# A two-layer mLSTM, sparse-attention and retention block: the mLSTM gate chain moved one section earlier, and evacuations given the weight chunks' priority

## The chip, the cores and the metric

The kernel runs on one core of one Trainium2 chip. The metric is the device time of one execution in microseconds (us); the time of a kernel is the median of its runs.

## What is computed

A sequence of 512 tokens of width 1024 goes through two layers. Each layer multiplies the normed tokens by one wide matrix `w_in`, cuts the result into the inputs of three mixers (an mLSTM, a sparse attention with an indexer, a retention), mixes, projects, and ends in a gated feed-forward block. Cut to what the change touches:

```python
h = rms_norm(x, norm1_g);  z = h @ w_in          # m_q m_k m_v m_i m_f m_o a_... r_... g_...
qk = silu(causal_conv(concat([m_q, m_k])))
# mLSTM gates, per head and token, in chunks of 128 tokens
log_f = log_sigmoid(m_f + m_fbias);  log_i = m_i + m_ibias
bcum = cumsum(log_f)                             # inside a chunk
m_row = max(bcum + m_state, max_r(bcum_l - bcum_r + log_i_r))
w_intra = exp(d_log - m_row);  w_inter = exp(bcum + m_state - m_row)
out = num / max(|den|, exp(-m_row));  m_state = max(b_last + m_state, max(g_log))
# indexer: 8 heads of scores that pick each token's keys
idx_sc = sum_g w_idx[g] * relu(q_idx[g] @ k_idx^T);  sel = top_k(idx_sc)
```

## The kernel before

All large products are made as three TensorE products of 32-bit halves (lines 251 to 253, `mm3`): a value x is held as a rounded part hi and a remainder lo, and hi*hi, hi*lo and lo*hi are added up in PSUM. Weights come in chunks of 256 rows by 512 columns (`chunk`, line 223): SP issues the load into `raw` (2 buffers), ACT writes `whi` (line 233), DVE subtracts to get `wlo` (line 234). `whi` and `wlo` have 3 buffers each. The whole of `chunk` is emitted under `tc.high_priority()`.

The work is written as sections, each 96 products of 512 columns into four `mm` PSUM tiles: `tok_section` (output rows are tokens) and `feat_section` (output rows are features). At its end a section calls `finish` (line 279), which evacuates the four tiles (on ACT or DVE, as the section says) and then runs the rest of each evacuation. The next section needs the same four PSUM tiles again.

Small work is fed in between: `self.feed` holds generators, and a section calls `tick` (line 116) eight times, which steps each generator by its rate. The program's order is only a start: Tile's scheduler orders each engine's instructions by priority and readiness, and `high_priority` lifts instructions. After that, every engine runs its list strictly in order and waits on semaphores.

The sections that matter here, in each layer: the misc section (the gate columns m_i, m_f, the indexer's inputs; line 413), QK (line 455), m_v (line 458), m_o (line 471), then r_q, r_k, r_v, r_g. Fed in between, before the change:

- in QK and m_v: `indexer` (line 607). For each of 4 head pairs `q_pair` (line 590) makes a product `sm`, from which ACT and DVE write the two `qs` tiles (lines 602, 603); for each head there are then six PE products (lines 623, 624), three ReLUs on ACT (line 626) and three accumulations into `mask` on DVE (lines 629, 631);
- in m_v: `conv_silu` (line 434): per feature tile one product and three shifted accumulations `cy` (lines 437, 440) on DVE, a Sigmoid on ACT (line 442), and `qz` or `kT` on DVE (lines 446, 448);
- in m_o: `mlstm_pre` (line 752) and `topk` (line 636), the latter at lowered priority. `mlstm_pre` begins with the gate chain: eight PE transposes of `gates` (lines 760, 761), 23 small DVE instructions on 4 partitions (lines 762 to 785), an Exp and a Ln on ACT (lines 765, 766) and, at the end, another Exp (line 787); then the PE transposes of the results A, nm and wl (line 793), the decay weights `mw` (lines 800 to 805), `qw` and `kw` (lines 811 to 823).

The small products use four `sm` PSUM tiles; POOL multiplies the four `og` tiles by the gain at the end of m_o (line 466).

Of the kernel before, what the change touches and what calls it, by code (L numbers as in the profile page):

```python
# [11 lines left out]
F32 = mybir.dt.float32  # L12
F32R = mybir.dt.float32r
AF = mybir.ActivationFunctionType
OP = mybir.AluOpType
# [88 lines left out]
class Block:  # L104
# [172 lines left out]
            self.finish(evac, [p[:, 0:n] for p in ps])  # L277

    def finish(self, evac, ps):
        rest = [evac(i, p) for i, p in enumerate(ps)]  # L280
        for f in rest:
            if f:
                f()
# [91 lines left out]
    def mixer(self, l, act):  # L375
        nc, a = self.nc, self.a
        w_in = a["w_in"][l]
        small = self.small[l]
        ib, conv = self.load_small(l)
# [3 lines left out]
        gates = self.st.tile([128, NT, 8], F32, name="gates", bufs=2)  # L383
# [37 lines left out]
        qz = self.b8("qz", [4, T])  # L421
# [32 lines left out]
        self.during((idx, 0.9), (bias, 0.6))  # L454
        self.feat_section(w_in, ((C_QK, C_QK + 512),), act, ev_qk)
        cs = conv_silu()
        self.feed.append([cs, 0.5, 0.0])
        self.tok_section(w_in, ((C_MV, C_MV + 512),), act, ev_v)
        self.drain(idx, bias, cs)

        mg = self.gain(a["m_norm_g"][l]).rearrange("p (h v) -> p h v", h=4)
        og = [self.r(f"og{t}", [4, 128]) for t in range(NT)]
# [2 lines left out]
            nc.scalar.activation(og[t], ps.rearrange("p (h v) -> p h v", h=4), AF.Sigmoid)  # L465
            nc.gpsimd.tensor_mul(og[t], og[t], mg)

        pre = self.mlstm_pre(l, gates, ib, qz, kT)
        top = self.topk(masks)
        self.during((pre, 1.0), (top, 1.0))  # L470
        self.tok_section(w_in, ((C_MO, C_MO + 512),), act, ev_og)
# [120 lines left out]
    def q_pair(self, W, f, CT, scale, t0):  # L592
        nc = self.nc
        p = self.sm()[:, 0:T - t0]
        for k in range(2):
            self.mm3(p, [x[:, k, f * 128:(f + 1) * 128] for x in W], [x[:, k, t0:] for x in CT], k == 0, k == 1)
        out = []
        for s in range(2):
            q = self.r("qs", dtype=F32R)
            d = q[:, t0:]  # L600
            hi, lo = (slice(0, 64), slice(64, 128))[::1 - 2 * s]
            nc.scalar.activation(d[hi], p[hi], AF.Copy, scale=scale)
            nc.vector.scalar_tensor_tensor(d[lo], p[hi], scale, d[hi].bitcast(F32), op0=OP.mult, op1=OP.subtract)
            out.append(q)
        return out

# [142 lines left out]
            self.to_T(ha[b].rearrange("p (f d) -> p f d", f=4), haT, b)  # L749
            yield  # L750

    def mlstm_pre(self, l, gates, ib, qz, kT):
        nc = self.nc
        g1, g2 = self.b8("g1", [4, T]), self.b8("g2", [4, T])
        li, fb, e, B = (g1[0:4, i, :] for i in range(4))
        A, M, nm, wl = (g2[0:4, i, :] for i in range(4))
        wi = e
        pi, pf = self.sm(), self.sm()
        for t in range(NT):
            nc.tensor.transpose(pi[0:4, t * 128:(t + 1) * 128], gates[:, t, 0:4], self.ident)  # L760
            nc.tensor.transpose(pf[0:4, t * 128:(t + 1) * 128], gates[:, t, 4:8], self.ident)
        nc.vector.tensor_scalar(li, pi[0:4], ib[:, 0:1], None, op0=OP.add)
        nc.vector.tensor_scalar(fb, pf[0:4], ib[:, 1:2], None, op0=OP.add)
        nc.vector.scalar_tensor_tensor(e, fb, -1.0, fb, op0=OP.mult, op1=OP.min)
        nc.scalar.activation(e, e, AF.Exp)
        nc.scalar.activation(e, e, AF.Ln, bias=1.0)
        nc.vector.scalar_tensor_tensor(fb, fb, 0.0, e, op0=OP.min, op1=OP.subtract)
        rows = [self.r("rows", parts=36, dtype=F32R) for _ in range(2)]
        for x in rows:
            nc.gpsimd.memset(x.bitcast(F32), 0.0)  # L770
        keep = self.r("keep", parts=4)
        nc.vector.memset(keep, 1.0)
        nc.vector.memset(keep[:, 0::128], 0.0)
        nc.vector.tensor_tensor_scan(B, keep, fb, 0.0, op0=OP.mult, op1=OP.add)
        nc.vector.tensor_sub(A, li, B)
        m = self.st.tile([4, NT + 1], F32, name="g_ms", bufs=2)
        nc.vector.memset(m[:, 0:1], 0.0)
        for c in range(NT):
            s = slice(c * 128, (c + 1) * 128)
            last = (c + 1) * 128  # L780
            nc.vector.tensor_tensor_scan(M[:, s], A[:, s], A[:, s], m[:, c:c + 1], op0=OP.max, op1=OP.max)
            nc.vector.tensor_add(m[:, c + 1:c + 2], B[:, last - 1:last], M[:, last - 1:last])
            nc.vector.tensor_scalar(wi[:, s], M[:, s], -1.0, m[:, c:c + 1], op0=OP.mult, op1=OP.add)
            nc.vector.tensor_scalar(wl[:, s], A[:, s], M[:, last - 1:last], None, op0=OP.subtract)
        nc.vector.scalar_tensor_tensor(nm, B, -1.0, M, op0=OP.mult, op1=OP.subtract)
        self.split(rows[0][0:4], rows[0][32:36], M)
        nc.scalar.activation(wi, wi, AF.Exp)
        self.split(rows[1][0:4], rows[1][32:36], wi)
        yield
        tok = self.sm([128, 3, NT, 4])  # L790
        for i, r in enumerate((A, nm, wl)):
            for c in range(NT):
                nc.tensor.transpose(tok[:, i, c, :], r[:, c * 128:(c + 1) * 128], self.ident[0:4, 0:4])
        G = self.st.tile([128, 3, NT, 4], F32, name="g_tok", bufs=2)
        nc.vector.tensor_copy(G[:, 0], tok[:, 0])
        nc.scalar.activation(G[:, 1:3], tok[:, 1:3], AF.Exp)
        W = self.b8("mw", [NT, 4, 128])
        for h in range(4):
            p = self.sm()
            nc.tensor.matmul(p, lhsT=self.sel[:, h:h + 1].to_broadcast([36, 128]), rhs=rows[0], start=True, stop=True)  # L800
            d = W[:, :, h, :]
            nc.vector.tensor_sub(d, self.negT[:, None, :].to_broadcast([128, NT, 128]),
                                 p.rearrange("p (c l) -> p c l", c=NT))
            for c in range(NT):
                nc.scalar.activation(W[:, c, h, :], W[:, c, h, :], AF.Exp, bias=G[:, 0, c, h:h + 1])
            yield
        qw = self.b8("qw", [4, T])
        dec = self.st.tile([128, 2, NT], F32, name="g_dec", bufs=2)
        for hp in range(2):
            p = self.sm()  # L810
            nc.tensor.matmul(p, lhsT=self.pair[:, hp * 128:(hp + 1) * 128], rhs=rows[1], start=True, stop=True)
            for s in range(2):
                nc.vector.tensor_mul(qw[:, 2 * hp + s, :], qz[:, 2 * hp + s, :], p)
            nc.vector.tensor_copy(dec[:, hp, :], p[:, 127::128])
            yield
        kw = [self.r(f"kw{c}", [4, 128]) for c in range(3)]
        for c in range(3):
            nc.gpsimd.memset(kw[c], 0.0)
            p = self.sm([128, 2, 2, 64])
            for hp in range(2):  # L820
                nc.tensor.transpose(p[:, hp].rearrange("p s d -> p (s d)"), kT[hp][:, c * 128:(c + 1) * 128], self.ident)
            for s in range(2):
                nc.vector.tensor_mul(kw[c][:, s::2, 64 * s:64 * s + 64], p[:, :, s, :],
                                     G[:, 2, c, s::2, None].to_broadcast([128, 2, 64]))
            yield
        self.ml = (W, G, qw, kw, dec)
# [196 lines left out]
```

## Time and profile before

| | us |
|---|---|
| median of 3 runs (lowest, highest) | 1836.69 (1836.31, 1838.33) |
| the profiled execution | 1840.39 |
| its span, first to last instruction | 1838.5 |
| PE busy in the span | 1803.9 (98%) |
| DVE busy | 985.8 (54%) |
| ACT busy | 733.1 (40%) |
| POOL busy | 215.1 (12%) |

Busy time of PE counts overlapping, pipelined products, so that 98% does not say that PE works at its peak; what PE waits for is read from its waits, and how fast it goes from the granted clock. "Idle before" in a row is the time in which the engine stood still just before that instruction, with what ended it.

### The profile page before, as it was taken

The numbers are of one execution on the slowest core, as the hardware profiler recorded it, in microseconds if no ns is written. First come the engines' busy times: TensorE is split into PE (matmuls) and PEld (weight loads), VectorE is DVE, ScalarE is ACT, GpSimd is POOL, SyncE is SP. The second block draws the span as 40 slices with busy tenths as digits, with TensorE's granted clock in tenths as the row PEclk, the third lists the DMA queues.
The fourth block names the chain that finished last, engine by engine and source line by source line (L and its number), as shares of the span: only waits on it lengthen the run. The fifth ranks groups of instructions, "written<-read, shape, count | busy, mean of one in ns | idle before, by whom it ended". The sixth has DMA issues, their size and how long they took to land.

```text
span 1838.5 us, 22889 instructions
## 1 busy us (share of the span) xinstructions
PE 1803.9 (98%) x8720; PEld 1497.9 (81%) x8720; DVE 985.8 (54%) x1798; ACT 733.1 (40%) x1202; POOL 215.1 (12%) x274
## 2 busy tenths in 40 slices
PE   9989999999999999999999899999999999999998
PEld 6868888878888888888888688888888888888886
DVE  5788985455555333322357889844546443333223
ACT  5553234656434233322246523356554342323221
POOL 3112240121000000000020131401210000000000
PEclk9989999999999999999999899999999999999999
DMA  5522423232235333222342223233223243332232
GB/s 186 201 85 65 119 75 98 84 94 88 81 126 149 104 92 101 94 94 102 101 130 81 63 81 103 65 98 94 89 70 120 98 150 103 92 101 94 92 103 81
DMA packets 126846, 185.95 MB, mean 101 GB/s; under 512 B 12257, under 2 KB 71137, under 8 KB 126737
## 3 DMA queue, kind: packets, MB, share of 16 engines
q1 hardware_dynamic: 125408, 178.98, 31.1%
q0 software_dynamic: 1184, 5.26, 0.8%
q8 instruction: 68, 1.11, 0.2%
q14 instruction: 42, 0.34, 0.1%
q10 hardware_dynamic: 144, 0.26, 0.0%
HBM read 177.64 MB, written 6.84 MB: 100 GB/s over the span
## 4 chain that ended last, share of the span: by engine, by line
PE 58%; DVE 7%; DMA 1%; ACT 1%; issue 1%; POOL 1%; SPq 0%; POOLq 0%; ACTq 0%; DVEq 0%
PE mm L253 18%; PE mm L251 18%; PE mm L252 18%; DVE wlo L234 2%; DVE mask L647 1%; DVE top L646 1%; PE sm L728 1%; DMA raw<-w_up 1%; PE sm L707 1%; ACT whi L233 1%; PE sm L721 0%; DVE ru L521 0%; PE sm L368 0%; POOL lnr L308 0%; PE sm L345 0%
## 5 line engine op out<-in xcount | busy, mean ns | idle before, releaser
L234 DVE TENSOR_TENSOR wlo<-raw,whi 128x1024 fp32r<-128x1024 f32 (+2 forms) x302 | 373.1, 1236 | 587.6 <-ACT whi L233 587.3
L233 ACT ACTIVATE whi<-raw 128x1024 fp32r<-128x1024 f32 (+2 forms) x302 | 313.9, 1040 | 727.8 <-PE mm L252 296.2
L251 PE MATMUL mm<-hT,whi 128*128 128x512 f32 (+1 forms) x1216 | 465.3, 383 | 1.6 <-ACT fg L956 1.6
L252 PE MATMUL mm<-hT,whi 128*128 128x512 f32 (+1 forms) x1216 | 460.4, 379 | 1.0 <-DVE hT L303 1.0
L253 PE MATMUL mm<-hT,wlo 128*128 128x512 f32 (+1 forms) x1216 | 460.8, 379 | 0.0
L253 PEld LDWEIGHTS mm<-hT,wlo 128*128 128x128 f32 x1216 | 228.7, 188 | 43.3 <-DVE wlo L234 0.2
L251 PEld LDWEIGHTS mm<-hT,whi 128*128 128x128 f32 x1216 | 228.9, 188 | 42.9 <-ACT fg L956 2.0
L252 PEld LDWEIGHTS mm<-hT,whi 128*128 128x128 f32 x1216 | 229.0, 188 | 42.0 <-DVE hT L303 1.6
L251 PE MATMUL mm<-whi,hT 128*128 128x512 f32 (+1 forms) x448 | 178.5, 399 | 1.0 <-ACT whi L233 0.4
L253 PE MATMUL mm<-whi,hT 128*128 128x512 f32 (+1 forms) x448 | 177.9, 398 | 0.0
L252 PE MATMUL mm<-wlo,hT 128*128 128x512 f32 (+1 forms) x448 | 176.9, 395 | 0.0
L253 PEld LDWEIGHTS mm<-whi,hT 128*128 128x128 f32 x448 | 85.8, 191 | 17.7 <-issue 0.9
L251 PEld LDWEIGHTS mm<-whi,hT 128*128 128x128 f32 x448 | 85.7, 191 | 17.7 <-ACT hT L302 1.4
L252 PEld LDWEIGHTS mm<-wlo,hT 128*128 128x128 f32 x448 | 85.7, 191 | 17.5 <-issue 1.3
L320 POOL TENSOR_SCALAR rs<-ms 128x1 f32<-128x1 f32 x16 | 5.7, 355 | 619.3 <-ACT hn L318 619.3
L253 PE MATMUL mm<-whi,fa 128*128 128x512 f32 x192 | 75.6, 394 | 0.0
L251 PE MATMUL mm<-whi,fa 128*128 128x512 f32 x192 | 75.5, 393 | 0.0
L252 PE MATMUL mm<-wlo,fa 128*128 128x512 f32 x192 | 75.5, 393 | 0.0
L709 POOL TENSOR_TENSOR cmb<-tb,mask 128x256 f32<-128x256 f32 (+2 forms) x48 | 52.0, 1088 | 163.1 <-DVE amx L712 74.3
L251 PE MATMUL mm<-whi,fr 128*128 128x512 f32 x160 | 62.4, 390 | 0.0
L253 PE MATMUL mm<-whi,fr 128*128 128x512 f32 x160 | 62.3, 389 | 0.0
L252 PE MATMUL mm<-wlo,fr 128*128 128x512 f32 x160 | 62.3, 389 | 0.0
(285 smaller groups left out, 2652.3 us busy)
## 6 DMA issues: line engine op xcount, KB each, us to landing
raw<-w_in SPq DMA_DIRECT2D x104, 512.0 KB, 3.6
raw<-w_gate SPq DMA_DIRECT2D x96, 256.0 KB, 2.9
raw<-w_up SPq DMA_DIRECT2D x96, 256.0 KB, 3.1
raw<-w_down SPq DMA_DIRECT2D x44, 512.0 KB, 3.5
raw<-w_out SPq DMA_DIRECT2D x16, 512.0 KB, 4.5
x<-x SPq DMA_DIRECT2D x8, 512.0 KB, 5.8
rot<-c_rot SPq DMA_DIRECT2D x16, 256.0 KB, 2.7
tb<-bias_dram SPq DMA_DIRECT2D x16, 256.0 KB, 3.4
```

Of the source, the lines that this page charges most:

```text
L233: nc.scalar.activation(h, r, AF.Copy)
L234: nc.vector.tensor_sub(o, r, h.bitcast(F32))
L251: t.matmul(out, lhsT=A[0], rhs=B[0], start=start, stop=False)
L252: t.matmul(out, lhsT=A[0], rhs=B[1], start=False, stop=False)
L253: t.matmul(out, lhsT=A[1], rhs=B[0], start=False, stop=stop)
L320: nc.gpsimd.tensor_scalar(r, ms[:, 0:1], ms[:, 1:2], EPS, op0=OP.add, op1=OP.add)
L646: nc.vector.max(m8, acc)
L647: nc.vector.match_replace(acc, m8, acc, TAKEN)
L707: nc.tensor.matmul(p, lhsT=q[v][:, b * 128:(b + 1) * 128], rhs=kk[v][:, 0:SP], start=v == 0, stop=v == 1)
L709: nc.gpsimd.tensor_add(c, tb[:, T - S:T], masks[b] if b else self.neg)
L728: nc.tensor.matmul(o[:, b, :], lhsT=PT[:, s, :], rhs=V[s][:, h * 64:(h + 1) * 64], start=s == 0, stop=s == b)
```

## The change

`mlstm_pre` is cut in two. Its first part, up to the split of the row tiles, becomes `mlstm_gates`, a generator with yields after the Ln, after A, and after each of the four chunks; it is fed at rate 1.0 in the m_v section (and drained after it), beside `indexer`, `bias_table` and `conv_silu`. The second part, from the transposes at line 793 on, stays in m_o. The arithmetic is the same. Besides, `finish` emits all evacuations under `tc.high_priority()`, and so does `q_pair` for its two evacuations.

```diff
     def finish(self, evac, ps):
-        rest = [evac(i, p) for i, p in enumerate(ps)]
+        with self.tc.high_priority():
+            rest = [evac(i, p) for i, p in enumerate(ps)]
...
         cs = conv_silu()
-        self.feed.append([cs, 0.5, 0.0])
+        rec = self.mlstm_gates(gates, ib)
+        self.feed += [[cs, 0.5, 0.0], [rec, 1.0, 0.0]]
         self.tok_section(w_in, ((C_MV, C_MV + 512),), act, ev_v)
-        self.drain(idx, bias, cs)
+        self.drain(idx, bias, cs, rec)
...
-        pre = self.mlstm_pre(l, gates, ib, qz, kT)
+        pre = self.mlstm_pre(qz, kT)
...
-            nc.scalar.activation(d[hi], p[hi], AF.Copy, scale=scale)
-            nc.vector.scalar_tensor_tensor(d[lo], p[hi], scale, d[hi].bitcast(F32), op0=OP.mult, op1=OP.subtract)
+            with self.tc.high_priority():
+                nc.scalar.activation(d[hi], p[hi], AF.Copy, scale=scale)
+                nc.vector.scalar_tensor_tensor(d[lo], p[hi], scale, d[hi].bitcast(F32), op0=OP.mult, op1=OP.subtract)
...
-    def mlstm_pre(self, l, gates, ib, qz, kT):
+    def mlstm_gates(self, gates, ib):
         nc = self.nc
+        yield
         g1, g2 = self.b8("g1", [4, T]), self.b8("g2", [4, T])
...
         nc.scalar.activation(e, e, AF.Ln, bias=1.0)
+        yield
...
         nc.vector.tensor_sub(A, li, B)
+        yield
...
             nc.vector.tensor_scalar(wl[:, s], A[:, s], M[:, last - 1:last], None, op0=OP.subtract)
+            yield
...
         self.split(rows[1][0:4], rows[1][32:36], wi)
-        yield
+        self.recur = (A, nm, wl), rows
+
+    def mlstm_pre(self, qz, kT):
+        nc = self.nc
+        (A, nm, wl), rows = self.recur
         tok = self.sm([128, 3, NT, 4])
```

What the scheduler makes of it, at three places. Line numbers of the change are higher than before by 1 to 11 (793 is 804 there, 602 is 605, 765 is 769).

PE, layer 0, around the transposes of the gate chain's last results (`sm<-cm,g`). Before, eight of the twelve stand behind the fifth product of r_q:

```order
L251 MATMUL mm<-whi,hT_117 128x512
L252 MATMUL mm<-wlo,hT_117 128x512
L793 MATMUL sm<-cm,g_1011 128x4 x8
L253 MATMUL mm<-whi,hT_119 128x512
L251 MATMUL mm<-whi,hT_117 128x512
L800 MATMUL sm<-rows,sel 128x512 x3
```

Now all twelve stand behind the 33rd product of m_o, just behind the indexer's last score products (lines 626, 627 of the change):

```order
L253 MATMUL mm<-whi,hT_119 128x512
L626 MATMUL sm<-CT_220,qs 128x384
L627 MATMUL sm<-CT_221,qs 128x384
L626 MATMUL sm<-CT_220,qs 128x512
L627 MATMUL sm<-CT_221,qs 128x512
L804 MATMUL sm<-cm,g_727 128x4 x12
L251 MATMUL mm<-whi,hT_117 128x512
```

They moved up by 68 products; the first four had stood behind the 74th product of m_o. In layer 1 four stand behind product 38 and eight behind product 57 of m_o, where they were behind 74 and 101. The eight transposes at the chain's head, which stood behind the 12th product of m_o, stand behind the 24th of m_v.

DVE, layer 0: the middle of the gate chain (`g`, `keep`), before, in the m_o section, among the first top-k steps (`top`, lines 646 and 647):

```order
L234 TENSOR_TENSOR wlo<-raw,whi 128x1024
L767 SCALAR_TENSOR_TENSOR g_1010<-g_1010 4x512
L647 MATCH_REPLACE mask_434<-top,mask_434 128x256
L774 SCALAR_TENSOR_TENSOR g_1010<-keep,g_1010 4x512
L646 MAX top<-mask_434 128x8
L775 TENSOR_TENSOR g_1011<-g_1010 4x512
L647 MATCH_REPLACE mask_434<-top,mask_434 128x256
L781 SCALAR_TENSOR_TENSOR g_1011<-g_1011,g_ms 4x128
```

and now, in the m_v section, among score accumulations (`mask`, line 634) and the remainders `qs` (line 606) of the indexer's third head pair:

```order
L234 TENSOR_TENSOR wlo<-raw,whi 128x1024
L772 SCALAR_TENSOR_TENSOR g_726<-g_726 4x512
L634 SCALAR_TENSOR_TENSOR mask_434<-relu,wgt,mask_434 128x256
L606 SCALAR_TENSOR_TENSOR qs<-sm,qs 64x384
L779 SCALAR_TENSOR_TENSOR g_726<-keep,g_726 4x512
L606 SCALAR_TENSOR_TENSOR qs<-sm,qs 64x384
L780 TENSOR_TENSOR g_727<-g_726 4x512
L634 SCALAR_TENSOR_TENSOR mask_435<-relu,wgt,mask_435 128x384
```

Top-k steps stand behind the whole chain now, and the chain stands ahead of and between the two `qs` tiles. Up to the chain's last instruction (line 785) DVE has, in layer 0, the same other work behind it as it had before up to the first `kT` (line 448); in layer 1 one `wlo`, two sets of three `mask` accumulations and a `cy` more.

ACT, layer 0, m_v section: the Exp and the Ln with their table loads now stand ahead of the evacuation of the third `qs` pair (line 605), which was preceded by ReLUs and a `whi` alone:

```order
L443 ACTIVATE cz<-cy 128x512
L629 ACTIVATE relu<-sm 128x256
L629 ACTIVATE relu<-sm 128x384
L629 ACTIVATE relu<-sm 128x512
L769 ACT_TABLE_LOAD
L769 ACTIVATE g_726<-g_726 4x512
L233 ACTIVATE whi<-raw 128x1024
L770 ACT_TABLE_LOAD
L770 ACTIVATE g_726<-g_726 4x512
L629 ACTIVATE relu<-sm 128x256
L629 ACTIVATE relu<-sm 128x384
L605 ACTIVATE qs<-sm 64x384 x2
```

The list of ACT has 49 table loads in place of 43, three more in each layer. Nothing else moves much: SP's list has layer 0's two loads of `rot` (256 KB each, line 505) moved from behind the misc section's chunks to ahead of its second and behind its third chunk, and in the attention some evacuations change places with their neighbours.

## Rows read from the trace of the kernel before

**Rows 1.** The page: its head.

```profile
span 1838.5 us, 22889 instructions
```

**Rows 2.** Waits of PE, whole span: waiter <- releaser: us in total, times, longest.

```profile
PE sm L793 <- DVE g L785: 7.3, 2, 3.6
...
PE sm L793 <- DVE g L775: 2.1, 2, 1.1
...
PE mm L251 <- ACT fg L956: 1.6, 1, 1.6
```

**Rows 3.** Timeline of PE, layer 0: start, duration, engine, line, out<-in [idle before <-releaser].

```profile
100.80 0.48 PE L251 MATMUL mm<-whi,hT 128*128 128x512 f32 x1
...
116.17 0.41 PE L793 MATMUL sm<-cm,g 4*128 4x4 f32 x4 [1.05 <-DVE g L775]
...
116.84 0.39 PE L251 MATMUL mm<-whi,hT 128*128 128x512 f32 x1
...
122.53 0.39 PE L252 MATMUL mm<-wlo,hT 128*128 128x512 f32 x1
126.55 1.00 PE L793 MATMUL sm<-cm,g 4*128 4x4 f32 x8 [3.63 <-DVE g L785]
```

**Rows 4.** Stretches, layer 0: length; busy PE, PEld, DVE, ACT, POOL (instructions); PEclk; DMA.

```profile
126.60:136.80 10.20, 10.20 (x27) 6.73 (x28) 6.45 (x13) 6.23 (x9) 1.28 (x1) 0.50 0.26 77
136.80:146.00 9.20, 9.20 (x54) 7.49 (x54) 6.65 (x17) 5.45 (x16) 0.00 (x0) 1.00 0.20 60
```

**Rows 5.** Stretch of layer 1 after its second such wait, same columns.

```profile
1034.50:1048.20 13.70, 12.44 (x32) 8.03 (x33) 7.73 (x18) 7.62 (x11) 1.28 (x1) 0.50 0.19 59
```

**Rows 6.** Timeline of PE and the stretch behind it, feed-forward part of layer 0.

```profile
586.15 0.50 PE L251 MATMUL mm<-hT,whi 128*128 128x512 f32 x1 [1.61 <-ACT fg L956]
...
587.00:600.00 13.00, 13.00 (x59) 10.66 (x58) 5.26 (x6) 3.36 (x5) 0.00 (x0) 1.00 0.54 161
```

**Rows 7.** Stretches of layer 0's gate chain, its own tile `g` alone (PE, PEld, DVE, ACT).

```profile
102.90:126.50 23.60, 0.41 (x4) 0.32 (x4) 12.56 (x23) 1.89 (x3) 1.00 0.23 67
118.50:123.40 4.90, 0.00 (x0) 0.00 (x0) 4.55 (x5) 0.00 (x0) 1.00 0.39 109
```

**Rows 8.** Timeline of DVE, layer 0.

```profile
82.41 0.55 DVE L603 SCALAR_TENSOR_TENSOR qs<-sm,qs 64x384 fp32r<-64x384 f32 x1
...
99.27 3.26 DVE L631 SCALAR_TENSOR_TENSOR mask<-relu,wgt,mask 128x256 f32<-128x256 f32 x6
...
118.54 1.31 DVE L784 TENSOR_SCALAR g<-g 4x128 f32<-4x128 f32 x1
...
124.40 0.27 DVE L784 TENSOR_SCALAR g<-g 4x128 f32<-4x128 f32 x1
...
125.83 0.67 DVE L785 SCALAR_TENSOR_TENSOR g<-g,g 4x512 f32<-4x512 f32 x1
```

**Rows 9.** Timeline of POOL, layer 0.

```profile
118.42 4.02 POOL L466 TENSOR_TENSOR og<-og,gain 128x512 f32<-128x512 f32 x3 [31.39 <-ACT og L465]
```

**Rows 10.** Stretch of layer 0 that the chain moves into, all engines as in rows 4.

```profile
70.30:99.27 28.97, 28.68 (x137) 24.03 (x136) 26.47 (x40) 18.25 (x33) 2.21 (x4) 1.00 0.44 147
```

**Rows 11.** Timeline of ACT, layer 0.

```profile
108.15 1.28 ACT L765 ACT_TABLE_LOAD   x1
109.44 0.63 ACT L765 ACTIVATE g<-g 4x512 f32<-4x512 f32 x1
```

**Rows 12.** Timeline of PE, layer 0: the third `qs` pair's first use.

```profile
83.15 0.28 PE L623 MATMUL sm<-CT,qs 128*128 128x256 f32 x1
```

**Rows 13.** Top-k's last step and its first reader, layer 0: durations, first and last start.

```profile
L647 DVE MATCH_REPLACE8 mask<-top,mask x48: 397/540/678, 109.9 to 243.6; 128x256 f32<-128x256 f32 x16, 128x384 f32<-128x384 f32 x16, 128x512 f32<-128x512 f32 x16
...
L709 POOL TENSOR_TENSOR cmb<-tb,mask x24: 724/1017/1992, 274.4 to 439.4; 128x256 f32<-128x256 f32 x8, 128x384 f32<-128x384 f32 x8, 128x512 f32<-128x512 f32 x8
```

**Rows 14.** Waits of PE's weight loads for an evacuation, whole span.

```profile
PEld mm L251 <- DVE sg L481: 1.0, 2, 0.5
```

**Rows 15.** The page: DMA issues, KB each, median us from issue to landing.

```profile
rot<-c_rot SPq DMA_DIRECT2D x16, 256.0 KB, 2.7
```

## The prediction

> **What bounds the kernel now.** I read the table of busy times first: PE is busy for 98% of the span of 1838.5 us [rows 1], DVE for 54%, ACT for 40%. So only what makes PE stand still, or go slowly, is worth time. The second view is PE's waits [rows 2]. The longest is for the gate chain, `sm L793 <- g`: 7.3 us and 2.1 us, each in two waits, one per layer, together 9.4 us. The next, 1.6 us, is in the feed-forward part and is not touched. The third view is PE's timeline in layer 0 [rows 3]: PE stands 1.05 us before the first four transposes and 3.63 us before the other eight. The fourth view, the stretches [rows 4, 5], shows what follows: right behind that second wait the granted clock is 0.50, the 1.2 GHz level, for 10.2 us in layer 0 and for some 13.7 us in layer 1, and then it is 1.00 again. PE is busy for 10.2 and 12.4 us of these, so half of that, 5.1 + 6.2 = 11.3 us, is lost to the clock. A wait of 1.61 us elsewhere is followed by a clock of 1.00 [rows 6]; so among these rows only the long wait was followed by the fall. What the chain costs today is 9.4 + 11.3 = 20.7 us.
>
> **Why the chain is late.** It is one dependent line on DVE, interleaved with top-k. Its 23 instructions take 12.56 us [rows 7]. Five of them, which run while POOL multiplies `og` [rows 9], take 4.55 us: a `g` subtraction of 0.27 us takes 1.31 us there [rows 8]. The undisturbed durations of the five, from the repeats of the same lines, add up to about 1.4 us, so that the chain by itself is 12.56 - 4.55 + 1.4 = 9.4 us.
>
> **The change part by part.**
>
> *The chain leaves m_o.* PE reaches its new place for the transposes after 33 products of m_o. Before, the 13th product started at 100.80, and a product takes (122.53 - 116.84) / 25 = 0.228 us [rows 3], so the 34th would start at 100.80 + 21 x 0.228 = 105.6 us. Nothing is added to PE: the eight head transposes are only earlier, and the time up to there is the same.
>
> When is DVE through? In layer 0 the order gives it, up to line 785, the same other work as it had done before at 99.27, when the last six `mask` steps began [rows 8]. To this the chain is added: 9.4 us, by which it would end at 99.27 + 9.4 = 108.7. DVE has holes in which some of it fits: in the 28.97 us up to 99.27 it was busy for 26.47 [rows 10], so at most 2.5 us are free. The chain then ends between 106.2 and 108.7, and if ACT's turns (the Exp and the Ln, each with a table load of 1.28 us [rows 11]) leave new holes as large as the old, at 108.7 or a little later. PE would be held up by 0.6 to 3.1 us. I take 2.4 us, nearer the upper end, because the chain goes through ACT and back twice and DVE has to wait for that in order. In layer 1 the order puts more other work ahead of line 785, some 5 us (six `mask` steps of 3.26 us together [rows 8], a `wlo` and a `cy`), but PE comes to the last eight transposes 24 products later, 24 x 0.228 = 5.5 us; so 2.4 us is taken there too. Together 4.8 us, between 1.2 and 6.2.
>
> PE need not lose this at the transposes. What is queued behind the chain on DVE and ACT are the `qs` tiles: the remainder of the third pair started at 82.41 and took 0.55 us [rows 8], and PE used it at 83.15 [rows 12], with 0.2 us to spare. Now two gate activations and two table loads on ACT and five gate instructions on DVE stand ahead of it. I expect the larger part of the wait there, at the indexer's score products, in the middle of m_v, and the rest in smaller pieces behind it, at the next pair and at the transposes.
>
> *The clock.* If the new waits are pieces of 1 to 2 us, they are nearer to the 1.61 us that left the clock alone [rows 6] than to the 3.63 us that did not [rows 3]. I take no fall: 11.3 us gained. The other end is 0.
>
> *Top-k* moves behind the chain. Its last step in layer 0 starts at 243.6 and its first reader on POOL at 274.4 [rows 13], so it has 30 us to spare and costs nothing. If it were late, POOL's `cmb` and the attention would wait.
>
> *POOL's `og` products* stay and now meet the `qw` and `kw` products and the weight remainders, where DVE would lose about the same 4.55 - 1.4 = 3.2 us per layer [rows 7]. Those feed the mLSTM's first chunk, which is fed into r_q with other products between. I take 0.5 us for both layers; the ends are 0 and 6.3.
>
> *Table loads.* Six more, 1.28 us each [rows 11], 7.7 us on an engine that is 40% busy. What of it is in front of PE is in the 2.4 us above; the rest is covered by ACT's idle time, and if it were not, the evacuations of m_o and so the first products of r_q would come late. The row shows the Exp starting at 109.44, as soon as the load that started at 108.15 is done [rows 11]. The Trainium skill (ScalarE: Activation LUTs, What ACT_TABLE_LOAD costs) gives about 1.28 us for the load and 1.38 us more of draining, 2.66 us for each switch, and advises to do all calls of one set before the next, which speaks against a change that adds switches. By the load as the rows show it the sum is the one below; by that price the rival on table loads holds.
>
> *Evacuations with priority.* The only wait of this kind on PE is 1.0 us in all [rows 14], so at most 1 us is to gain; as much could be lost in the attention, whose instructions step back. I take 0. One evacuation closure issues the load of `rot`, and in layer 0 two of them move to the first misc chunks on SP's queue. Each lands in 2.7 us [rows 15] and may hold up the second chunk by anything from 0 to that; I take 0, since that chunk's evacuation stands behind the row norms on ACT anyway.
>
> **The sum.** 9.4 + 11.3 - 4.8 - 0.5 = 15.4 us less. The profiled execution took 1840.4 us with a span of 1838.5, so it would take 1825.0. It lies 3.7 us above the median of the three runs, 1836.7; 15.4 us below that median is **1821.3 us**.
>
> **The rivals.**
>
> 1. *Clean.* DVE's holes take up the chain and no new wait comes: 20.7 us less, 1816.0. For it: DVE idles 2.5 us in that stretch [rows 10]. Against it: the chain is 9.4 us, and 0.2 us of slack at the third `qs` pair. Chance 0.11.
> 2. *The clock still falls in one layer.* The new wait is in one piece of 2.4 us or more, which lies between the wait that left the clock alone and the one that did not. 5.6 us come back: 1826.9. Chance 0.16. In both layers: 11.3 us back, 1832.6. Chance 0.10.
> 3. *Slower: the whole chain lands on PE.* All 9.4 us per layer stand on DVE in front of a `qs` tile that PE needs at once, nothing is hidden, and the clock falls as before. New waits of 18.8 us take the place of 9.4, so 1836.7 + 9.4 = 1846.1. It decides from the point at which the new waits are larger than the old ones and still end in a half clock. For it: DVE is 91% busy there [rows 10]. Against it: PE goes on with weight products until the next `qs`, and the chain is spread between them by its yields. Chance 0.04.
> 4. *Table loads cost double.* Were ACT blocked for about as long again behind each load, 1.3 us more for the two loads ahead of the third `qs` pair, that is 2.6 us per layer, come on to PE: 5.2 us back, 1826.5. Against it is the start of the Exp at 109.44 [rows 11]. Chance 0.02. The Trainium skill (ScalarE: Activation LUTs, What ACT_TABLE_LOAD costs) is what would make it so; the trace disagrees with that price.
> 5. *It does not act.* The scheduler's new places bring as much wait as before, with the same clock: 1836.7. Against it: the order shows the chain's head 84 products earlier, 84 x 0.228 = 19 us. Chance 0.02.
>
> **How the numbers follow.** The forecast has what is left, 0.55. A measurement can tell about 0.2%, 3.7 us, from no change. Faster by more than that, under 1833.0: the forecast, the clean case, one falling clock, the table loads, and half of the case of two falling clocks, which lies on the border: 0.55 + 0.11 + 0.16 + 0.02 + 0.05 = 0.89. Within: 0.05 + 0.02 = 0.07. Slower: 0.04. The range reaches from the clean case with 3 us of better evacuations and mLSTM waits, 1813, to one falling clock with the upper end of the new waits and 2.7 us for `rot`, 1831. It leaves out two falling clocks, the fifth rival and the slower one, 0.16.
>
> **What would show it.** In the changed kernel's profile: PE's wait at the transposes of `g` under 1 us per layer; new waits at the score products for `qs` or for a `relu`, 1 to 2 us each, some 5 us over both layers; the granted clock 1.00 from m_v through r_q in both layers; the `g` instructions of 4 x 128 all near 0.27 us; 49 table loads of 1.28 us. It is wrong if a stretch at 0.50 stands in m_v or m_o, if one wait of PE is over 3 us, or if PE waits in r_q for `mw`, `qw` or an `og` evacuation by several us.

## The result and the profile after

The changed kernel takes 1827.92 us (median of 4 runs, 1826.73 to 1828.15), the kernel before, on the same chip, 1837.51 (1836.31 to 1839.80): a ratio of 0.9944, 95% interval 0.9932 to 0.9955. That is faster, by 9.6 us at the medians, where 15.4 were forecast; the time lies inside the range and 6.6 us above the forecast. The two profiled executions, 1840.39 and 1827.70 us, are 12.7 us apart.

The page of the changed kernel: its head, PE's busy time, and the granted clock in 40 slices.

```profile
span 1825.9 us, 22880 instructions
...
PE 1796.5 (98%) x8720; PEld 1490.9 (82%) x8720; DVE 982.5 (54%) x1798; ACT 741.1 (41%) x1208; POOL 217.5 (12%) x274
...
PEclk9999999999999999999999999999999999999999
```

PE stands still for 1825.9 - 1796.5 = 29.4 us instead of 1838.5 - 1803.9 = 34.6, and is busy for 7.4 us less. The next fence holds PE's waits over the whole span (total, times, longest), as [rows 2] does for before.

```profile
PE sm L626 <- DVE qs L606: 2.2, 2, 1.6
PE sm L626 <- ACT relu L629: 2.1, 2, 1.3
PE sm L710 <- ACT kk L692: 2.0, 4, 0.8
...
PE mm L251 <- ACT hT L303: 1.3, 1, 1.3
PE sm L873 <- DVE msc L852: 1.1, 2, 0.9
...
PE mm L251 <- ACT fg L967: 0.2, 1, 0.2
```

The transposes of the chain (L804 now) are no longer in the list. New or longer are the score products' waits for `qs` (0.7 us in before) and for a `relu`, and, in the attention, four waits for `kk`, while two for `prob`, 1.3 us in all in before, are gone. The wait for `fg` [rows 6] has fallen from 1.6 to 0.2 us. PE's timeline in layer 0 shows the first change and the new places: 1.56 us in m_v at the third pair, and in m_o the transposes directly behind the last score products.

```profile
86.24 0.38 PE L626 MATMUL sm<-CT,qs 128*128 128x256 f32 x1 [1.56 <-DVE qs L606]
...
108.43 0.44 PE L626 MATMUL sm<-CT,qs 128*128 128x384 f32 x1 [0.81 <-ACT relu L629]
...
109.46 0.71 PE L804 MATMUL sm<-cm,g 4*128 4x4 f32 x9
```

The stretches of [rows 4, 5] at the same times, all engines: the granted clock is 1.00, the 2.4 GHz level, where two of the three stood at 0.50.

```profile
126.60:136.80 10.20, 10.20 (x56) 8.75 (x55) 9.15 (x30) 10.07 (x17) 6.30 (x5) 1.00 0.30 93
136.80:146.00 9.20, 8.34 (x54) 7.18 (x53) 8.00 (x32) 2.95 (x8) 1.27 (x2) 1.00 0.21 66
1034.50:1048.20 13.70, 13.45 (x88) 11.76 (x87) 12.46 (x49) 5.61 (x15) 1.45 (x3) 1.00 0.27 80
```

In the stretch of the chain, of its own tile `g` alone (PE, PEld, DVE, ACT), 23 DVE instructions take 9.92 us, against 12.56 in [rows 7]: away from `og` the chain is nearly as short as the 9.4 us worked out. Its last instruction ends at 108.66 us, at the upper end of the 106.2 to 108.7 worked out.

```profile
73.50:108.80 35.30, 0.00 (x0) 0.00 (x0) 9.92 (x23) 1.26 (x2) 1.00 0.34 106
```

ACT's timeline in layer 0 shows why the third pair is late. Exp and Ln of the chain each load a table, and the `qs` copy, which DVE and PE wait for, starts only at 85.14, behind both; before, its remainder on DVE already ran at 82.41 [rows 8].

```profile
79.31 1.28 ACT L769 ACT_TABLE_LOAD   x1
80.60 0.63 ACT L769 ACTIVATE g<-g 4x512 f32<-4x512 f32 x1
...
82.20 1.28 ACT L770 ACT_TABLE_LOAD   x1
83.49 0.63 ACT L770 ACTIVATE g<-g 4x512 f32<-4x512 f32 x1
...
85.14 0.46 ACT L605 ACTIVATE qs<-sm 64x384 fp32r<-64x384 f32 x1
```

### The profile page after: what moved, and what is told of

Same layout as the page of the kernel before. It is cut to its first block, busy times and chain, and to the rows that moved or that the text cites. A ratio compares the mean times of both kernels' runs of the same rounds, so it can differ in the third digit from the quotient of the medians.

```text
span 1825.9 us, 22880 instructions
## 1 busy us (share of the span) xinstructions
PE 1796.5 (98%) x8720; PEld 1490.9 (82%) x8720; DVE 982.5 (54%) x1798; ACT 741.1 (41%) x1208; POOL 217.5 (12%) x274
## 4 chain that ended last, share of the span: by engine, by line
PE 78%; DVE 14%; ACT 3%; DMA 2%; issue 2%; POOL 1%; SPq 0%; POOLq 0%; ACTq 0%; DVEq 0%
PE mm L251 23%; PE mm L253 23%; PE mm L252 23%; DVE wlo L234 3%; DVE mask L650 3%; DVE top L649 2%; PE sm L731 2%; PE sm L710 1%; ACT whi L233 1%; PE sm L724 1%; DMA raw<-w_up 1%; DVE ru L523 1%; PE sm L369 1%; DVE mhx L362 0%; DMA uk<-a_wuk 0%
## 5 line engine op out<-in xcount | busy, mean ns | idle before, releaser
L251 PE MATMUL mm<-whi,hT 128*128 128x512 f32 (+1 forms) x448 | 177.2, 396 | 2.0 <-ACT hT L303 1.3
L253 PE MATMUL mm<-whi,hT 128*128 128x512 f32 (+1 forms) x448 | 174.6, 390 | 0.0
```

The source lines that it names most:

```text
L251: t.matmul(out, lhsT=A[0], rhs=B[0], start=start, stop=False)
L253: t.matmul(out, lhsT=A[1], rhs=B[0], start=False, stop=stop)
```

## The experiments

The theory at the start: the gain is the chain's move; PE's long wait at the transposes and the half clock behind it are gone, the priorities are worth little, and what is lost again are the waits at the score products. The first rival: the priorities bring a large part. The second, about the cause: the chain is not long by itself but slowed by POOL's `og` products, so that it need not move at all.

| kernel | median us | ratio to before, 95% interval |
|---|---|---|
| the whole change | 1827.92 | 0.9944, 0.9932 to 0.9955 |
| gates_only | 1833.35 | 0.9975, 0.9966 to 0.9984 |
| prio_only | 1839.18 | 1.0006, 0.9997 to 1.0015 |
| gates_finish | 1826.99 | 0.9939, 0.9927 to 0.9951 |
| gates_qpair | 1833.00 | 0.9971, 0.9960 to 0.9982 |
| no_gain_before | 1821.72 | 0.9917, 0.9903 to 0.9930 |
| long_chain | 1830.75 | 0.9968, 0.9957 to 0.9979 |
| log_sigmoid | 1825.13 | 0.9935, 0.9923 to 0.9948 |
| gates_in_qk | 1829.39 | 0.9957, 0.9945 to 0.9970 |
| gain_late | 1827.97 | 0.9946, 0.9934 to 0.9959 |
| gain_late_log | 1829.08 | 0.9956, 0.9943 to 0.9968 |
| gain_late_mv | 1835.42 | 0.9989, 0.9980 to 0.9998 |
| gain_behind | 1820.73 | 0.9915, 0.9902 to 0.9929 |

### The parts of the change, four kernels

gates_only: the change with the gates in m_v and both priorities taken out.

```diff
-        with self.tc.high_priority():
-            rest = [evac(i, p) for i, p in enumerate(ps)]
+        rest = [evac(i, p) for i, p in enumerate(ps)]
...
-            with self.tc.high_priority():
-                nc.scalar.activation(d[hi], p[hi], AF.Copy, scale=scale)
...
+            nc.scalar.activation(d[hi], p[hi], AF.Copy, scale=scale)
```

> The gate chain is fed in the m_v section; both priorities are taken out. Theory (the move of the chain is the change, the priorities are small): the granted clock is 1.00 from m_v to r_q in both layers, PE has no wait at the transposes of the chain, and the time is 1829 to 1831, about 8 us under the kernel before; the waits of 1.6 us on the fg evacuation and 1.0 us on an sg evacuation, which the whole change lost, are back. Rival (the chain in m_v only pays if the qs and the evacuations go first): waits for qs of over 3 us in m_v, the clock falls behind them, and the time is 1834 or more.

gates_qpair: the first of these two edits alone.

> The whole change without the priority of the evacuations. Theory: the waits for fg (1.6 us) and sg (1.0 us) are back: 1829.5 to 1831. Rival (the priority of the evacuations costs as much elsewhere: the first chunks at the start, the late mw Exps in layer 0 behind two alternating activation tables): the same as the whole change or faster, 1826 to 1828.

gates_finish: the second alone.

> The whole change without the priority of the q tiles. Theory: the third qs pair, behind the chain on ACT and DVE, comes later by the instructions that now go first, so PE waits for it 1 to 2 us more per layer than in the whole change: 1829 to 1831. Rival (the scheduler finds the same order without it): the same as the whole change, 1827.9 within 0.8.

prio_only: the kernel before with both priorities added.

> The kernel before with both priorities and the gate chain left where it was. Theory: the two long waits for the chain in m_o and the half clock behind them stay, and only the waits for fg and sg go, some 2 us: 1835 to 1836.5. Rival (the priorities bring a large part of the gain): under 1833.

Measured: without the evacuations' priority the move is worth only some 5 us (1833.35 and 1833.00); with it, and without the priority of the q tiles, 1826.99. On its own the priority brings nothing (1839.18). So the first theory fails in one part: the evacuations' priority is worth 5 to 6 us, though only once the chain has moved (ratios of 0.9971 without it and 0.9944 with it, intervals apart). That the q tiles' priority is worth anything the intervals do not show. The theories on the single kernels missed: gates_only lies between its theory and its rival, gates_qpair is 2 us above its theory, gates_finish is under its theory and near its rival, although its longest wait for `qs` did grow, from 1.6 to 2.1 us, and prio_only gained none of the 2 us that were expected, although the wait for `fg` is gone there. One thing that the priority costs shows in the attention: PE waits 2.1 us for `kk` in prio_only and 1.6 in gates_finish, as in the whole change, and 1.3 us for `prob` instead in before, gates_only and gates_qpair.

In gates_qpair the waits that decide are new ones at the end of m_o. Its waits of PE:

```profile
PE mm L251 <- ACT og L466: 3.5, 2, 2.0
...
PE sm L859 <- DVE kw L833: 1.4, 1, 1.4
```

PE's timeline there, in layer 0, the first product of r_q:

```profile
132.24 0.50 PE L251 MATMUL mm<-whi,hT 128*128 128x512 f32 x1 [1.99 <-ACT og L466]
```

ACT's timeline of the same kernel:

```profile
124.10 3.62 ACT L815 ACTIVATE mw<-mw,g_tok 128x128 f32<-128x128 f32 x12
...
129.03 1.26 ACT L815 ACTIVATE mw<-mw,g_tok 128x128 f32<-128x128 f32 x4
130.29 1.28 ACT L466 ACT_TABLE_LOAD   x1
131.59 2.06 ACT L466 ACTIVATE og<-mm 128x512 f32<-128x512 f32 x4
```

And its stretch right behind (length; busy PE, PEld, DVE, ACT, POOL; PEclk; DMA):

```profile
133.10:136.50 3.40, 3.40 (x10) 2.62 (x9) 1.92 (x7) 0.56 (x2) 3.40 (x5) 0.50 0.10 33
```

The 16 `mw` Exps, which had to wait for the chain before, are now ready in m_o. Without the priority they and a table load stand ahead of the four `og` evacuations, which hold PE's four product tiles; PE waits 1.99 us, and the clock falls for 3.4 us. In layer 1 the same comes behind a wait for `kw`. In the whole change `og` goes first, at a price: ACT changes its table five times within 11 us. Its timeline in the whole change:

```profile
122.92 1.28 ACT L816 ACT_TABLE_LOAD   x1
...
124.63 1.28 ACT L467 ACT_TABLE_LOAD   x1
...
127.52 1.28 ACT L816 ACT_TABLE_LOAD   x1
...
130.19 1.28 ACT L467 ACT_TABLE_LOAD   x1
...
132.10 1.28 ACT L816 ACT_TABLE_LOAD   x1
...
135.09 3.61 ACT L816 ACTIVATE mw<-mw,g_tok 128x128 f32<-128x128 f32 x12
```

The last twelve Exps end at 138.7, where in gates_qpair the last ones ended at 130.3, and PE waits up to 0.9 us for `msc` (above): the cheaper wait.

### Why the chain was late in m_o: no_gain_before

```diff
-            nc.gpsimd.tensor_mul(og[t], og[t], mg)
+            pass
```

> The kernel before, in the same order on PE, DVE and ACT around the gate chain, without POOL's eight products of og with the norm's gain: the output lacks that gain. Theory (DVE and POOL slow each other; the clock falls only behind a wait of PE that is long): the instructions of the chain beside og take 0.27 and 0.47 us instead of up to 1.59, the chain ends some 3 us earlier in each layer, the second wait of PE falls from 3.6 to about 0.5 us, the clock stays at 1.00, and 6 + 11 = 17 us are gained: 1820 to 1822, under both kernels. Rival 1 (the chain was slow by itself): its instructions and the waits stay, 1837. Rival 2 (the clock falls for another reason than the length of the wait, as the many small transposes there): the waits shrink, the clock still falls to 0.50 for 10 to 14 us, 1831.

Measured: 1821.72, as the theory had it, and under both kernels, with the chain in its old place. DVE's timeline, where [rows 8] had 1.31 us:

```profile
118.66 0.27 DVE L784 TENSOR_SCALAR g<-g 4x128 f32<-4x128 f32 x1
```

PE's waits of this kernel for the chain:

```profile
PE sm L793 <- DVE g L775: 2.1, 2, 1.1
...
PE sm L793 <- DVE g L785: 0.4, 2, 0.2
```

The 7.3 us have become 0.4, the first wait of 2.1 us is unchanged, and the granted clock shows no 0.50 ahead of the last 3.3 us, where every kernel here has some. The span is 18.6 us shorter: 6.9 of waits and 11.3 of half clock make 18.2. Both rivals fall: the chain is not slow by itself, and here the transposes without the long wait leave the clock alone.

### Can the gain be multiplied in later? gain_late, gain_late_log, gain_late_mv, gain_behind

gain_late: the kernel before, with POOL multiplying the gain into the normalised heads.

```diff
-            nc.gpsimd.tensor_mul(og[t], og[t], mg)
...
             self.head_norm(hx, og[c])
+            nc.gpsimd.tensor_mul(hx, hx, mg)
```

> The kernel before, chain left in m_o and no priority; POOL multiplies the norm's gain into the normalised heads of each mLSTM chunk, instead of into og while the chain runs. Theory (the whole loss came from POOL's products beside the chain): the chain's instructions take 0.27 and 0.47 us, the clock stays at 1.00, and it is about as fast as the kernel without the gain, 1821.7: 1820 to 1824. Rival (the same eight products cost DVE and the mLSTM's chunks as much in r_q, or each chunk's way to PE gets 1.3 us longer and PE waits for hmT): 1826 or more.

gain_late_log adds the evacuations' priority and the log of a Sigmoid (the diff of log_sigmoid, below):

> As the one with the late gain, chain in m_o, and also the evacuations' priority and the log of a Sigmoid in the chain. Theory (the wait of 1.05 us at the first transposes in each layer comes from the chain's length, and the fg wait from the evacuations' order): another 2 to 3 us less, 1817 to 1820. Rival (in m_o the og Sigmoids and the chain's Ln alternate the tables, and the evacuations' priority is worth nothing without the chain in m_v, as measured): the same as the late gain alone, within 1.5.

gain_late_mv is the change with the late gain and the log of a Sigmoid, without the q tiles' priority:

> The changed kernel with the late gain and the log of a Sigmoid, without the q tiles' priority. Theory (in the new place POOL's og products meet only work with slack, so taking them away there gains less than 1 us; the log of a Sigmoid gains 2.8, and the q tiles' priority costs 0.9): 1823 to 1825. Rival (the products beside qw, kw and the weight remainders are what is left of the loss): under 1821.

All three miss: 1827.97, 1829.08, 1835.42. In gain_late the chain's second wait is down to 0.3 us in all, as the theory had it, but the POOL product now stands between the head norm and the transposes of `hmT`, a path with less slack than I took it to have. PE's waits in gain_late:

```profile
PE sm L368 <- POOL mhx L871: 2.3, 2, 1.1
PE sm L861 <- DVE msc L840: 2.3, 2, 1.2
```

PE's waits in gain_late_log:

```profile
PE sm L369 <- POOL mhx L870: 7.5, 2, 3.8
```

and the stretch of gain_late_log behind the first of these:

```profile
175.70:179.10 3.40, 3.40 (x10) 2.68 (x9) 0.00 (x0) 0.60 (x1) 2.21 (x4) 0.50 0.66 189
```

The wait is this long because the fourth of these products is slow itself. POOL's timeline in gain_late_log, the third and the fourth:

```profile
163.03 1.30 POOL L870 TENSOR_TENSOR mhx<-mhx,gain 128x512 f32<-128x512 f32 x1 [2.49 <-DVE mdn L864]
...
171.24 3.92 POOL L870 TENSOR_TENSOR mhx<-mhx,gain 128x512 f32<-128x512 f32 x1 [2.50 <-DVE mhx L364]
```

Beside the fourth, DVE makes `ru`, `rq`, `ru` and `wlo`, each from two SBUF tiles and in its usual time (0.69 and 1.22 us). In gain_late the fourth takes 2.79 us, in gain_late_mv 3.92; in gain_late and gain_late_log the other three take 1.26 to 1.30. So the late gain meets again what it was to avoid, POOL and DVE slowing each other, this time with POOL as the one that waits. This is read from the timelines; no run isolates it.

So the rival held for gain_late. For gain_late_log the rival's time held, not its reason. What POOL's products cost in the whole change was the question of gain_late_mv; its own new wait, 7.6 us, hides that, and it stays open.

gain_behind leaves the product on `og`, on POOL, before the heads are needed, and makes it start behind the chain: a zero worked out from the chain's result is added to the gain first.

```diff
-            nc.gpsimd.tensor_mul(og[t], og[t], mg)
...
         self.drain(pre)
+        zero = self.st.tile([128, 1], F32, name="g_zero", bufs=2)
+        nc.gpsimd.tensor_scalar(zero, self.ml[1][:, 0, 0, 0:1], 0.0, None, op0=OP.mult)
+        nc.gpsimd.tensor_scalar(mg, mg, zero, None, op0=OP.add)
+        for x in og:
+            nc.gpsimd.tensor_mul(x, x, mg)
```

> The kernel before, chain in m_o and no priority, with POOL's eight products of og with the gain still made, but held back until the chain is through: the gain tile first gets a zero added that is worked out from the chain's result, so the products can start only behind it. Theory (the same products harm only beside the chain): the chain is as fast as without them, PE's second wait under 0.5 us, the clock 1.00, and what they now slow on DVE, the mw differences, qw and kw, costs PE up to 1 us per layer: 1821.5 to 1824, under the changed kernel. Rival (the products are only moved to the next thing that PE waits for, as the late gain was, now msc or kw): waits for these grow by 2 us or more per layer, 1826 or more.

Measured: 1820.73, a little under the theory's range, and with no_gain_before the fastest kernel of this study: 5 us under the whole change by the ratios to before, 7 by the medians, without moving the chain or any priority. POOL's timeline:

```profile
128.12 6.50 POOL L476 TENSOR_TENSOR og<-og,gain 128x512 f32<-128x512 f32 x4
```

DVE's timeline beside it:

```profile
130.58 1.29 DVE L817 TENSOR_TENSOR qw<-qz,sm 128x512 f32<-128x512 f32 x2 [0.90 <-PE sm L815]
131.79 1.67 DVE L234 TENSOR_TENSOR wlo<-raw,whi 128x1024 fp32r<-128x1024 f32 x1
```

Of what runs beside the same four products now, only the `wlo` remainder is clearly longer (1.67 against some 1.2 us); the `mw` differences ended at 127.65, ahead of them. Nothing that PE waits for is late.

### What the new waits in m_v hang on: log_sigmoid, gates_in_qk, long_chain

log_sigmoid, on the whole change:

```diff
-        nc.vector.scalar_tensor_tensor(e, fb, -1.0, fb, op0=OP.mult, op1=OP.min)
-        nc.scalar.activation(e, e, AF.Exp)
-        nc.scalar.activation(e, e, AF.Ln, bias=1.0)
+        nc.scalar.activation(e, fb, AF.Sigmoid)
+        nc.scalar.activation(fb, e, AF.Ln)
         yield
-        nc.vector.scalar_tensor_tensor(fb, fb, 0.0, e, op0=OP.min, op1=OP.subtract)
```

> The changed kernel with log of the forget gate as Ln of a Sigmoid, instead of a product with minimum, Exp, Ln of one plus it, and a subtraction: two DVE instructions of 0.67 us and, where a Sigmoid table is already loaded, one or two table loads less in each layer ahead of the third qs pair. Theory (the new waits for qs and relu come from the chain's instructions and table loads ahead of them on ACT and DVE): those waits, 4.3 us over both layers, fall to under 2: 1824 to 1826.5. Rival (they come from the order of the score products itself): they stay, 1827.9 within 0.8.

Measured: 1825.13, in the theory's range, 2.8 us under the whole change by the medians (the intervals of the ratios overlap). Its waits of PE at the score products:

```profile
PE sm L626 <- DVE qs L606: 1.6, 1, 1.6
...
PE sm L251 <- ACT relu L629: 0.9, 1, 0.9
...
PE sm L626 <- ACT relu L629: 0.4, 2, 0.2
```

These make 2.9 us instead of 4.3: less, but not under 2. The chain's length and loads account for part of them; one wait of 1.6 us has only moved on to a later pair.

gates_in_qk, on the whole change:

```diff
-        self.during((idx, 0.9), (bias, 0.6))
+        rec = self.mlstm_gates(gates, ib)
+        self.during((idx, 0.9), (bias, 0.6), (rec, 0.5))
...
-        self.feed += [[cs, 0.5, 0.0], [rec, 1.0, 0.0]]
+        self.feed.append([cs, 0.5, 0.0])
```

> The changed kernel with the chain fed one section earlier, at the q and k of the mLSTM, at half the rate. Theory: the chain's Exp and Ln are through before the third qs pair, whose wait goes (1.6 us at most per layer), and the chain ends earlier than its transposes; but the indexer's own transposes and first qs pairs have the chain in front of them: 1825 to 1829. Rival (DVE is filled there, and each instruction of the chain only pushes another in front of PE): waits for qs or hT grow by 2 to 4 us per layer, 1831 or more.

Measured: 1829.39, just above the theory's range: no better place than m_v. Its waits of PE, and the stretch that begins within the first, in the slowest of its five executions (the mean granted clock is 0.995 there, 0.997 or 0.998 in the others):

```profile
PE sm L626 <- ACT relu L629: 3.2, 2, 2.4
...
PE mm L251 <- ACT cz L432: 2.4, 1, 2.4
```

```profile
69.60:76.40 6.80, 5.35 (x14) 4.48 (x15) 3.46 (x8) 4.81 (x11) 1.32 (x2) 0.50 0.94 340
```

long_chain, on the whole change:

```diff
         nc.vector.tensor_sub(A, li, B)
+        for _ in range(10 if l else 5):
+            nc.vector.tensor_scalar(A, A, 0.0, None, op0=OP.add)
         yield
```

> The changed kernel with additions of zero put into the chain on DVE, one behind the other, 5 in layer 0 and 10 in layer 1, 0.27 to 0.7 us each, that is up to 3.4 and 6.8 us; the value is the same. Theory: the transposes move back by some products, PE's new waits grow by 1 to 3 us in layer 0 and 2 to 5 in layer 1; where a single wait is over 3 us the clock falls to 0.50 behind it and some 5 us more are lost: 1831 to 1840. Rival (DVE's holes and the moved transposes take it up): the same as the changed kernel, 1827.9 within 1.5, clock 1.00.

Measured: 1830.75, between the two. In layer 0 the scheduler moves the transposes back and no long wait comes; in layer 1 a wait for `g_dec` takes their place. The clock falls twice in layer 1, once 13 us before that wait ends and once within it. The profiled execution, 1834.42 us, is the slowest of six. PE's wait, and the stretches:

```profile
PE sm L834 <- DVE g_dec L827: 2.1, 1, 2.1
```

```profile
1020.80:1027.70 6.90, 6.90 (x16) 4.79 (x16) 4.88 (x9) 1.25 (x2) 0.00 (x0) 0.51 0.09 22
...
1034.50:1041.30 6.80, 4.95 (x12) 3.68 (x13) 5.17 (x17) 6.74 (x14) 4.23 (x4) 0.50 0.26 80
```

The additions took 0.41 us each, so 2.0 us more were hidden in layer 0, and 4.1 us more were not wholly hidden in layer 1.

## Why the prediction was right, and where it was not

- *The chain's waits, 9.4 us.* Right: none of them is left.
- *The clock, 11.3 us.* Right in kind: 1.00 from m_v through r_q in both layers. The step to it, that waits of 1 to 2 us leave the clock alone, is no rule, and in part it was luck: in other kernels the clock fell at waits of 1.3 to 2.1 us (last section). The size was that of one execution. no_gain_before gains 18.6 us against the profiled execution of before, but 15.3 at the medians (1837.06 to 1821.72). The waits are 6.9 of it, so that at the medians the clock is worth about 8.4 us, an estimate from these two numbers. The granted clock of before says the same: 0.993 on average over the eleven runs beside no_gain_before, 0.992 in the profiled execution, a difference of some 2 us of lost clock. The kernels whose record holds no half clock scatter by 1.3 to 1.5 us over 4 to 5 runs; before lies between 1835.1 and 1842.2, over many more runs. Taking 11.3 us off a median was the step that was mis-sized, by some 3 us of the 6.6. Another 0.8 is the fourth run of before, with which its median is 1837.51 and no longer 1836.69.
- *New waits, 4.8 us.* Right in place and about in size: waits for `qs` rose from 0.7 to 2.2 us and for `relu` from none to 2.1, together 3.6; the largest is 1.6, and no clock falls behind it.
- *Evacuation priority, 0 (at most 1 us either way).* This is the step that failed. I priced it by what the kernel before showed [rows 14]. With the chain moved, the `mw` Exps compete with `og`, and the priority is worth 5.1 us (1833.00 to 1827.92), half of the gain. The prediction had named late evacuations of m_o, but under the table loads, as covered by ACT's idle time; without the priority they cost PE 3.5 us of waits and two stretches of half clock. That the time lies inside the range in spite of this is luck: the change holds the cure for a loss that the sum did not have.
- *The wait for `fg`.* I called it the next one and not touched. In total the waits for `rsc` (2.6 us) and `hn` (2.4) are longer, and it fell by 1.4 us. In the kernels with the moved chain and without the evacuations' priority it is 0.5 and 0.9, in no_gain_before 0.6, and in gain_behind it is gone, so part of the 1.6 was that execution's own.
- *POOL's `og` in the new place, 0.5 us.* In the chain nothing is slowed much (9.92 us). In the new place one `mask` step took 1.27 us instead of 0.27, and the POOL product beside a `wlo` 2.06 instead of 1.26; the price was not isolated.
- *Table loads.* 49, as forecast, 1.28 us each, the Ln at 83.49 right behind the load of 82.20. But gates_only and gates_qpair have 43, as before, and prio_only has 39: the six more come of the move and the evacuations' priority together, and the prediction had put none of them down to the priority. The 2.66 us for a switch that the Trainium skill gives (ScalarE: Activation LUTs, What ACT_TABLE_LOAD costs) are not seen: the activation starts 1.29 us after the load does, and the load 0.02 us after the activation before it ends. The advice of the Trainium skill to do all calls of one set together (ScalarE: Activation LUTs, Table sets: the hidden batching unit) fits log_sigmoid, which has 47 loads and is 2.8 us faster by the medians; but it saves two DVE instructions as well, and the intervals overlap.
- *`rot` at the start, 0.* About right. PE waits 1.3 us for `hT` there, 0.4 in before, but what comes behind the wait starts at 11.10 instead of 10.89, only 0.2 us later: the wait is longer because the products ahead of it were done earlier. gain_late, where the loads of `rot` stand as in before, waits 1.45 us and goes on at 10.95.
- *The rest.* By the profiled executions 12.7 of 15.4 us came. PE's standing fell by 5.2 us; 9.4 - 4.8 - 0.5 = 4.1 were forecast, and the 1.4 for `fg`, which were not, make it 5.5; its busy time fell by 7.4, not 11.3. In no_gain_before, with the same clock, it fell by 10.1. The 2.7 us between are in products that run less densely in the new order; no view names a cause, and it stays open.

Of the rivals, none came, though the second's and the fourth's times, 1826.9 and 1826.5, are near the one measured: no half clock and no longer table switch is there. The fall of the clock that the second rests on came in gates_only and gates_qpair, for 3.4 to 6.8 us each, that is 1.7 to 3.4 us lost and not the 5.6 priced. What I did not weigh is that the 4.55 us beside `og` [rows 7] were the cause: without them the wait of 3.6 us is gone where it stood.

## What to carry to other kernels

Before moving a late chain, look at what runs beside it on another engine, and whether its instructions take longer there than elsewhere: here the cure was to hold back four POOL products, the first by 10 us. When work moves earlier, ask what it releases earlier and whose queue that then heads; a priority that is worth nothing before the move can be worth half the gain behind it. And a stretch of half clock seen in one execution is not a price for the median.

## What the runs showed of the hardware that was not expected

*DVE beside POOL.* Three of the four POOL products slowed DVE by 3.2 us beside the chain; all four, beside the work behind it, by some 0.5. Slowed were the `g` instructions (scans and additions of two SBUF tiles, and additions of a scalar to one), a `mask` step on two SBUF tiles in the whole change (1.27 against 0.27 us), and `wlo`; not slowed were `qw` and `kw`, which read one of their inputs from PSUM, nor the top-k steps. It goes the other way too: beside DVE's `ru`, `rq` and `wlo` a POOL product of 1.30 us took 2.79 and 3.92 us (gain_late, gain_late_log). The Trainium skill (SBUF — State Buffer, Who interferes with whom) says that DVE contends with GpSimd where it has two SBUF inputs or is in a 2-port mode, and not otherwise, and that whoever issues first has the shared ports for its whole instruction. The rows agree: L784 became 1.04 us longer [rows 8], less than the 1.34 us of one POOL product [rows 9], and `qw` stayed at 0.64. Which mode an instruction was in, no trace shows.

*The clock behind a wait.* Waits of PE, and the length of the stretch at 0.50 that began close to the wait's end, ahead of it or behind it; each entry is one execution:

| wait of PE, us | kernels | length at 0.50, us |
|---|---|---|
| 1.3 to 1.7, for the first `hT`, at 11 us | gates_only, gates_in_qk, gain_late, gain_late_log, gain_late_mv | 3.4 each |
| 0.3 to 1.3, at the same place | the nine other kernels | none |
| up to 1.6, alone, later | the whole change, log_sigmoid, gain_behind | none |
| 2.06, at the third `qs` pair | gates_only | 3.4 |
| 2.06, at the third `qs` pair | gates_finish | none |
| 1.99, at `og` | gates_only and gates_qpair | 3.4 each |
| 1.4 and 1.55, 2.7 us apart | gates_only and gates_qpair, layer 1 | 6.8 and 3.4 |
| 2.06, at `g_dec` | long_chain | 6.8 |
| 2.4 | gates_in_qk, twice | 6.8 and 3.4 |
| 2.4, at `rsc` | gain_late_mv | none |
| 3.7 to 3.9, at `mhx` | gain_late_log, gain_late_mv | 3.4, 3.4, 3.4, 6.8 |
| 3.6, at the chain | before and prio_only, two each | 10.2, 13.7, 17.1, 10.2 |

The same wait of 2.06 us at the same product left the clock alone in one kernel and not in the other, and at the start 1.30 us (the whole change) left it alone where 1.33 (gates_in_qk) did not. PE's timeline in gates_finish:

```profile
88.80 0.39 PE L625 MATMUL sm<-CT,qs 128*128 128x256 f32 x1 [2.06 <-DVE qs L605]
```

PE's timeline in gates_only, where a product takes 0.63 us right behind:

```profile
88.67 0.39 PE L624 MATMUL sm<-CT,qs 128*128 128x256 f32 x1 [2.06 <-DVE qs L604]
...
89.85 0.63 PE L251 MATMUL mm<-whi,hT 128*128 128x512 f32 x1
```

Nor does the length follow from the wait: at the chain it was 10 us and more, at `mhx` 3.4 to 6.8. In long_chain the clock fell at 1020.8 with no PE wait over 0.3 us in the 5 us ahead; in its last 2 us stand the twelve small transposes of the chain and products of 36 rows. In the whole change the same twelve at 109.46 left the clock alone. What else decides is open.
